# Gated unit of a streaming encoder layer: where ScalarE's operand splits stand among the sigmoids

## The chip, the cores and the metric

The kernel runs on one core of a Trainium2 chip. The metric is the device time of one execution in microseconds. The core has TensorE for matmuls (PE in the profile; PEld is its weight load), VectorE (DVE), ScalarE (ACT), GpSimd (POOL) and SyncE (SP), which here issues the DMAs. Each engine works through its own queue in order.

## The reference

One layer of a hybrid encoder is computed for a prompt of 1024 frames and for 8 x 16 sample frames, 1152 tokens of 1024 features in all. Windowed attention and a state space recurrence (S5) run side by side, and then a convolutional feed-forward network. The change lies in the end of the S5 branch, the gated unit, and in the output projection behind it. Cut to these:

```
z = gelu(y)                                   # (tokens, 512)
s = z * sigmoid(z @ w_glu)                    # w_glu (512, 512)
merged = concat([rmsnorm(a, g_a), rmsnorm(s, g_s)])
x = x + merged @ w_out                        # w_out (1024, 1024)
x = x + conv_ffn(rmsnorm(x))
```

## The kernel before

Everything is float32. Each large product is made of three matmuls on fp32r operands: an operand is split into a high part (a ScalarE copy, rounded to fp32r) and a low part (VectorE, the operand minus its high part), and `mm3` (L60) adds high by high, low weight by high and high by low. In the trace, VectorE's subtraction has line L86, a helper's, and the three matmuls L61, L62 and L63.

The gated unit, `glu(nb)` (L1160), treats the 1152 tokens in three groups of 384. For a group it needs the split of its part of `zT`: `z_tiles` (L942) makes the tiles `zh` and `zlo`, `z_split` (L946) fills them for a slice of the four 128-row blocks, with one ScalarE instruction (L948) and one of VectorE. For each of four output blocks `fo`, 12 matmuls (`pg`) go to a PSUM tile; blocks 0 and 2 use the pool `psc` and blocks 1 and 3 the pool `pat`, two banks each. ScalarE takes the sigmoid of it (`sg`, L1172), which frees the bank; `SG[nb, fo]` keeps that instruction. VectorE multiplies by `zT`, ScalarE makes the high part (`sh`, L1174), VectorE the low part (`sl`), and ScalarE squares (`sqs`, L1177, or in place, L1179), with VectorE adding the squares up. The tile `sg` has two buffers, so the third sigmoid needs the first block's readers to be done. At the end six tiny matmuls (`pss`, L1181) sum the squares into a `psc` bank, and VectorE makes the reciprocal root `rss` from them in twelve small steps.

The first group's splits stand in `y_T` (L995), each behind the gelu of its rows. The second group's tiles lie in a pool of their own, `zl1`; the third group's reuse the first's, in `zl0`.

`load_wo(1, ...)` (L686) makes the operands of the lower half of the output weights: four rows of blocks are loaded (`wor`, tag `xs`, three buffers), and each gives a high part scaled by the norm's gain (`oh`, ScalarE, L704) and a low part (`ol`, VectorE, L705). `wout_s(t)` (L1207) multiplies a tile of 128 tokens by them: two halves of 12 matmuls (`po`) each, evicted by VectorE into the residual `xs` (L1219), then a norm (L1226 to L1229). `h2_T` (L1232) transposes the result (`h2T`) and prepares the operands `hh` of the up-projection (`pu`), whose weights `load_up` (L1276) brings into `ur` and `prep` (L1290) splits into `op`. Those tiles lie where the gated unit's inputs lay.

The text of the program is an order of wishes: the builder's planner puts each engine's instructions in a fixed order of its own, by what is ready when in its plan. `tc.issue_after(ins)` binds it: whatever the block holds for the engine of `ins` (here ScalarE, since `ins` is a sigmoid) is placed behind `ins` in that engine's queue. It adds no wait on the data, and it binds no other engine: VectorE's low parts and SP's loads are free.

The lines around the change are in `emit` itself:

```
    z_tiles(1, zlp)
    for k in range(4):
        z_split(1, slice(k, k + 1))
...
    glu(0)
    with tc.issue_after(SG[0, 0].ins):
        WO[1] = load_wo(1, wop, wk, "xs", 3)
        z_tiles(2, zl0)
        z_split(2, slice(0, 4))
    glu(1)
    glu(2)
```

Of the kernel before, what the change touches and what calls it, by code (L numbers as in the profile page):

```python
# [45 lines left out]
def emit(ctx, tc, x_prompt, x_sample, cache_k, cache_v, state_ssm_re, state_ssm_im, state_conv,  # L46
# [10 lines left out]
    def f(ap):  # L57
        return ap.bitcast(F32)

    def mm3(out, lh, ll, rh, rl, first, last):  # L60
        mm(out, lh, rh, start=first, stop=False, skip_group_check=True)  # L61
        mm(out, lh, rl, start=False, stop=False, skip_group_check=True)  # L62
        return mm(out, ll, rh, start=False, stop=last, skip_group_check=True)  # L63

    def mmf(out, l, r, first=True, last=True):
        mm(out, l, r, start=first, stop=last, skip_group_check=True)

    def pool(name, bufs=1, **kw):
        return tc.tile_pool(name=name, bufs=bufs, reuse_waits="tile", **kw)
# [15 lines left out]
    def tt(o, a, b, op):  # L85
        V_.tensor_tensor(o, a, b, op=op)  # L86
# [23 lines left out]
    def rstd(pl, out, src, width, more=None):  # L110


        n = out.shape[1]
        i = nid()
        a, b, t = (pl.tile([P, n], F32, name=f"rs{c}{i}", tag=f"rs{c}{n}", bufs=1) for c in "abt")
        y = pl.tile([P, n], I32, name=f"rsy{i}", tag=f"rsy{n}", bufs=1)

        def mul(o, x, z, s2=None, op1=None):

            if n == 1:  # L120
                ts(o, x, z, OP.mult, s2, op1)
            else:
                tt(o, x, z, OP.mult)
                if s2 is not None:
                    tt(o, o, s2, op1) if not isinstance(s2, float) else ts(o, o, s2, op1)

        if more is None:
            ts(a, src, 1.0 / width, OP.mult, EPS, OP.add)
        else:
            stt(a, src, 1.0 / width, more, op0=OP.mult, op1=OP.add)  # L130
        ts(y, a.bitcast(I32), -0.5, OP.mult, 1597463007.0, OP.add)
        c = f(y)
        mul(t, c, c, a, OP.mult)
        ts(t, t, -0.5, OP.mult, 1.50087896, OP.add)
        tt(b, c, t, OP.mult)
        mul(t, b, b, a, OP.mult)
        ts(y.bitcast(F32), t, 0.375, OP.mult, -1.25, OP.add)
        mul(t, c, t, 1.875, OP.add)
        tt(out, b, t, OP.mult)
# [546 lines left out]
    def load_wo(part, wp, rawp, tag, bufs):  # L686
        oh = wp.tile([P, 4, DM], F32R, name=f"oh{part}", tag="oh")
        ol = wp.tile([P, 4, DM], F32R, name=f"ol{part}", tag="ol")
        g = consts.tile([P, 4], F32, name=f"og{part}")
        if part == 0:  # L690
            for kv in range(KVH):
                nc.sync.dma_start(g[kv * 64:kv * 64 + 64],
                                  onorm_attn_g[0].rearrange("(k r d) -> k d r", r=RQ, d=HD)[kv])
        else:
            nc.sync.dma_start(g, onorm_ssm_g[0].rearrange("(k p) -> p k", p=P))
        for r in range(4):
            raw = rawp.tile([P, DM], F32, name=f"wor{part}{r}", tag=tag, bufs=bufs)
            if part == 0:
                src = w_out[0, 0:512].rearrange("(k r d) n -> r k d n", r=RQ, d=HD)
                for kv in range(KVH):  # L700
                    nc.sync.dma_start(raw[kv * 64:kv * 64 + 64], src[r, kv])
            else:
                nc.sync.dma_start(raw, w_out[0, 512 + r * P:512 + (r + 1) * P])
            act(oh[:, r], raw, AF.Copy, scale=g[:, r:r + 1])  # L704
            stt(ol[:, r], raw, g[:, r:r + 1], f(oh[:, r]), op0=OP.mult, op1=OP.subtract)  # L705
        return oh, ol
# [235 lines left out]
    def z_tiles(nb, pl):  # L942
        ZH[nb] = pl.tile([P, 4, NBK], F32R, name=f"zh{nb}", tag="zh", bufs=1)
        ZL[nb] = pl.tile([P, 4, NBK], F32R, name=f"zlo{nb}", tag="zl", bufs=1)

    def z_split(nb, ks):  # L946
        tk = slice(nb * NBK, (nb + 1) * NBK)
        act(ZH[nb][:, ks], zT[:, ks, tk], AF.Copy)  # L948
        tt(ZL[nb][:, ks], zT[:, ks, tk], f(ZH[nb][:, ks]), OP.subtract)
# [185 lines left out]
    zl0 = wxa.enter_context(pool("zl0"))  # L1135
# [15 lines left out]
    zl1 = ExitStack()  # L1151
    zlp = zl1.enter_context(pool("zl1", side="right"))
    z_tiles(1, zlp)
    for k in range(4):
        z_split(1, slice(k, k + 1))
    g2 = consts.tile([P, KD], F32, name="g2")
    nc.sync.dma_start(g2, norm2_g[0].rearrange("(k p) -> p k", p=P))
    SB, SG = {}, {}

    def glu(nb):  # L1160
        tk = slice(nb * NBK, (nb + 1) * NBK)
        sh = sgp.tile([P, 4, NBK], F32R, name=f"sh{nb}", tag="sh")
        sl = sgp.tile([P, 4, NBK], F32R, name=f"sl{nb}", tag="sl")
        sqr = sgp.tile([P, NBK], F32, name=f"sqs{nb}", tag="sqs", bufs=1)
        for fo in range(4):
            pl, tg = ((psc, "sc"), (pat, "at"))[fo % 2]
            ps = pl.tile([P, NBK], F32, name=f"pg{nb}{fo}", tag=tg)
            c = slice(fo * P, (fo + 1) * P)
            for k in range(4):
                mm3(ps, gh[:, k, c], gl[:, k, c], ZH[nb][:, k], ZL[nb][:, k], k == 0, k == 3)  # L1170
            sg = sgp.tile([P, NBK], F32, name=f"sg{nb}{fo}", tag="sg")
            SG[nb, fo] = act(sg, ps, AF.Sigmoid)  # L1172
            tt(sg, zT[:, fo, tk], sg, OP.mult)
            act(sh[:, fo], sg, AF.Copy)  # L1174
            tt(sl[:, fo], sg, f(sh[:, fo]), OP.subtract)
            if fo == 0:
                act(sqr, sg, AF.Square)  # L1177
            else:
                act(sg, sg, AF.Square)  # L1179
                tt(sqr, sqr, sg, OP.add)  # L1180
        pss = psc.tile([P, 3], F32, name=f"pss{nb}", tag="sc")  # L1181
        for i in range(3):
            mmf(pss[:, i:i + 1], sqr[:, i * P:(i + 1) * P], ones)
        rss = sgp.tile([P, 3], F32, name=f"rss{nb}", tag="rss")
        rstd(sgp, rss, pss, 512)
        SB[nb] = (sh, sl, rss)
# [72 lines left out]
        nc.gpsimd.tensor_tensor(o, a, b, op=op)  # L1259

    glu(0)
    with tc.issue_after(SG[0, 0].ins):
        WO[1] = load_wo(1, wop, wk, "xs", 3)
        z_tiles(2, zl0)
        z_split(2, slice(0, 4))
    glu(1)
    glu(2)
    zl1.close()
    wxa.close()
# [509 lines left out]
```

## Time and profile before

| | |
|---|---|
| median of 3 runs | 1221.35 us (1220.76 to 1225.33) |
| the profiled execution | 1222.4 us, of which the span of its instructions is 1220.5 |
| mean granted TensorE clock | 0.983 |
| TensorE busy | 1162.7 us, 95% of the span |
| VectorE, ScalarE, GpSimd busy | 940.5, 657.6, 253.6 us |
| first matmul of the gated unit | 342.3 us |
| last matmul of the gated unit | about 397 us |
| TensorE idle from 340 to 460 us, by what it waited for | VectorE's eviction `xs` 5.6 us in 2 waits; `sh` 2.5; `op` 2.3; `st` 1.6; `zT` 1.5 in 2; `sl` 0.8; `sg` 0.6 |

Times in a timeline count from the first instruction. A row has the start, the duration (or the sum of the merged ones, from the first's start to the last's end), the engine, the line, what is written from what, the shape and the count; in brackets stand the idle time of the engine just before and the instruction that ended it. Matmuls overlap, so the distance between two starts, not the duration, is the price of one. The rows of windows hold the busy time of each engine in a stretch, the granted clock, the share of the DMA engines and the bytes per second.

### The profile page before, as it was taken

To read this page: it belongs to the slowest core of one execution; us is meant where nothing else is said; L and a number is where in the kernel's file an instruction comes from. 1 tells how busy PE (TensorE), PEld (TensorE's weight loads), DVE (VectorE), ACT (ScalarE), POOL (GpSimd) and SP (SyncE) were. 2 spreads that over 40 slices of the span, in tenths; PEclk is the share of its full clock that TensorE was granted. 3 is DMA by queue.
4 is the path that set the end of the run, shared out by engine and by line. 5 is a ranking of instruction groups with operands and counts; after the bars stand their busy time and mean duration, and the time that the engine had idled before them with its cause. 6 is when DMAs were issued, how large, how long until landed. Compare 5 with 4: busy or idle time off the path is not lost. (4 is left out here: it accounts for less than half of the span.)

```text
span 1220.5 us, 20645 instructions
## 1 busy us (share of the span) xinstructions
PE 1162.7 (95%) x7396; PEld 1024.4 (84%) x7396; DVE 940.5 (77%) x2058; ACT 657.6 (54%) x1414; POOL 253.6 (21%) x287
## 2 busy tenths in 40 slices
PE   8999999899979887999999999999999998999996
PEld 6777776677769667999999999999999776888885
DVE  6898868797446878887877878878878678977665
ACT  7346556763385766544545445445454555446553
POOL 0000000000000102554454645535443014000000
PEclk9999999999999989999999999999999999999998
DMA  8523236658722421324434334244342799842333
GB/s 264 102 85 123 92 73 195 208 180 234 215 96 86 155 87 52 124 90 143 124 106 145 107 127 140 90 136 132 109 141 99 238 332 343 281 145 94 96 103 138
DMA packets 165032, 177.89 MB, mean 146 GB/s; under 512 B 30618, under 2 KB 122402, under 8 KB 164898
## 3 DMA queue, kind: packets, MB, share of 16 engines
q1 hardware_dynamic: 164930, 176.58, 45.4%
q8 instruction: 58, 0.95, 0.3%
q14 instruction: 44, 0.36, 0.1%
HBM read 124.36 MB, written 53.23 MB: 146 GB/s over the span
## 5 line engine op out<-in xcount | busy, mean ns | idle before, releaser
L1304 DVE TENSOR_TENSOR op<-ur,op 128x512 fp32r<-128x512 f32 x132 | 121.0, 918 | 87.2 <-ACT op L1303 87.1
L1303 ACT ACTIVATE op<-ur 128x512 fp32r<-128x512 f32 x132 | 83.1, 632 | 96.7 <-POOL ur L1259 43.7
L1259 POOL TENSOR_TENSOR S<-ur 128x512 f32<-128x512 f32 x22 | 43.7, 1984 | 242.3 <-DMA ur<-in_w_up_dram 242.1
L1527 ACT ACTIVATE wh<-wd 128x512 fp32r<-128x512 f32 x110 | 68.4, 628 | 26.6 <-PE dnb L63 7.0
L86 DVE TENSOR_TENSOR wl<-wd,wh 128x512 fp32r<-128x512 f32 x110 | 76.3, 704 | 5.9 <-ACT wh L1527 5.7
L62 PE MATMUL dna<-wl,gh 128*128 128x512 f32 x176 | 69.3, 394 | 0.0
L61 PE MATMUL dna<-wh,gh 128*128 128x512 f32 x176 | 64.2, 396 | 3.5 <-ACT wh L1527 3.5
L1392 POOL COPY cvt<-ext 128x2 f32<-128x2 f32 x44 | 30.3, 689 | 158.4 <-DVE ext L86 158.4
L63 PE MATMUL dna<-wh,gl 128*128 128x512 f32 x176 | 54.6, 392 | 0.0
L86 DVE TENSOR_TENSOR gl<-gr,gh 128x512 fp32r<-128x512 f32 x44 | 31.4, 713 | 28.6 <-PE dna L63 12.0
L62 PE MATMUL dnb<-wl,gh 128*128 128x512 f32 x132 | 50.3, 392 | 3.0 <-DVE wl L86 3.0
L86 DVE TENSOR_TENSOR ws<-ws 128x256 f32<-128x256 f32 x88 | 51.8, 589 | 0.7 <-DMA ws<-in_w_down_dram 0.6
L61 PE MATMUL dnb<-wh,gh 128*128 128x512 f32 x132 | 49.0, 392 | 0.6 <-DVE x L86 0.6
L1527 ACT ACTIVATE gh<-gr 128x512 fp32r<-128x512 f32 x44 | 27.6, 630 | 34.7 <-PE dna L62 21.7
L1393 POOL COPY cvt<-ext 128x16 f32<-128x16 f32 x44 | 32.8, 746 | 61.2 <-ACT ext L1363 61.2
L1396 DVE SCALAR_TENSOR_TENSOR cg<-ext,cw,cg 128x1168 f32<-128x1168 f32 x22 | 43.5, 1978 | 0.0
L61 PEld LDWEIGHTS dna<-wh,gh 128*128 128x128 f32 x176 | 33.0, 189 | 11.4 <-ACT wh L1527 4.5
L1527 ACT ACTIVATE gh<-su 128x512 fp32r<-128x512 f32 x33 | 20.9, 632 | 36.8 <-PE dnb L62 13.5
L62 PEld LDWEIGHTS dna<-wl,gh 128*128 128x128 f32 x176 | 33.4, 190 | 7.5 <-DVE wl L86 0.4
L63 PEld LDWEIGHTS dna<-wh,gl 128*128 128x128 f32 x176 | 33.5, 190 | 7.0
L1259 POOL TENSOR_TENSOR ur<-S,ur 128x512 f32<-128x512 f32 x22 | 35.8, 1626 | 17.2 <-DVE op L1304 17.1
L61 PE MATMUL po<-oh,sh 128*128 128x512 f32 x72 | 31.1, 431 | 8.1 <-DVE xs L1219 5.6
(1278 smaller groups left out, 4336.9 us busy)
## 6 DMA issues: line engine op xcount, KB each, us to landing
ur<-in_w_up_dram SPq DMA_DIRECT2D x44, 512.0 KB, 4.7
wd<-in_w_down_dram SPq DMA_DIRECT2D x66, 256.0 KB, 3.5
ws<-in_w_down_dram SPq DMA_DIRECT2D x44, 256.0 KB, 3.4
g_d<-g SPq DMA_DIRECT2D x22, 512.0 KB, 2.6
t_d<-ws SPq DMA_DIRECT2D x22, 512.0 KB, 3.2
gr<-g_d SPq DMA_DIRECT2D x44, 256.0 KB, 6.0
wd<-t_d SPq DMA_DIRECT2D x44, 256.0 KB, 3.0
wa<-a_d SPq DMA_DIRECT2D x9, 512.0 KB, 3.4
```

The lines of the kernel that those rows point to most:

```text
L61: mm(out, lh, rh, start=first, stop=False, skip_group_check=True)
L62: mm(out, lh, rl, start=False, stop=False, skip_group_check=True)
L63: return mm(out, ll, rh, start=False, stop=last, skip_group_check=True)
L86: V_.tensor_tensor(o, a, b, op=op)
L1259: nc.gpsimd.tensor_tensor(o, a, b, op=op)
L1303: act(op[:, 0], src, AF.Copy)
L1304: LOW[n] = V_.tensor_tensor(op[:, 1], src, f(op[:, 0]), op=OP.subtract)
L1392: nc.gpsimd.tensor_copy(cvt[:, 0:2, ft], ext[:, SEQ:SEQ + 2])
L1393: nc.gpsimd.tensor_copy(cvt[:, 2:, ft].rearrange("p (b j) -> p b j", j=2), es[:, :, NS:])
L1396: stt(o, ext[:, 0:GLEN], cw[:, 0, ft:ft + 1], o, op0=OP.mult, op1=OP.add)
L1527: act(hi, src, AF.Copy)
```

## The change

Three blocks of ScalarE and VectorE work are moved in the program's text. The second group's split, four pieces, was traced before the first group's unit and free to run when its data was there; it is now traced behind `glu(0)` and bound behind the second sigmoid of the first group. The output weights' operands were bound behind the first sigmoid and are now bound behind the fourth. The third group's split stood in the same place as the weights, as one instruction for all four row blocks; it now stands behind `glu(1)`, in four pieces, bound behind the second sigmoid of the second group.

```
--- before.py
+++ after.py
@@ -1151,8 +1151,6 @@
     zl1 = ExitStack()
     zlp = zl1.enter_context(pool("zl1", side="right"))
     z_tiles(1, zlp)
-    for k in range(4):
-        z_split(1, slice(k, k + 1))
     g2 = consts.tile([P, KD], F32, name="g2")
     nc.sync.dma_start(g2, norm2_g[0].rearrange("(k p) -> p k", p=P))
     SB, SG = {}, {}
@@ -1259,11 +1257,16 @@
         nc.gpsimd.tensor_tensor(o, a, b, op=op)
 
     glu(0)
-    with tc.issue_after(SG[0, 0].ins):
+    with tc.issue_after(SG[0, 1].ins):
+        for k in range(4):
+            z_split(1, slice(k, k + 1))
+    with tc.issue_after(SG[0, 3].ins):
         WO[1] = load_wo(1, wop, wk, "xs", 3)
-        z_tiles(2, zl0)
-        z_split(2, slice(0, 4))
     glu(1)
+    z_tiles(2, zl0)
+    with tc.issue_after(SG[1, 1].ins):
+        for k in range(4):
+            z_split(2, slice(k, k + 1))
     glu(2)
     zl1.close()
     wxa.close()
```

The functions that the text names, with the lines of the profile:

```
 942    def z_tiles(nb, pl):
 943        ZH[nb] = pl.tile([P, 4, NBK], F32R, name=f"zh{nb}", tag="zh", bufs=1)
 944        ZL[nb] = pl.tile([P, 4, NBK], F32R, name=f"zlo{nb}", tag="zl", bufs=1)
 945
 946    def z_split(nb, ks):
 947        tk = slice(nb * NBK, (nb + 1) * NBK)
 948        act(ZH[nb][:, ks], zT[:, ks, tk], AF.Copy)
 949        tt(ZL[nb][:, ks], zT[:, ks, tk], f(ZH[nb][:, ks]), OP.subtract)
...
1165        for fo in range(4):
1166            pl, tg = ((psc, "sc"), (pat, "at"))[fo % 2]
1167            ps = pl.tile([P, NBK], F32, name=f"pg{nb}{fo}", tag=tg)
1168            c = slice(fo * P, (fo + 1) * P)
1169            for k in range(4):
1170                mm3(ps, gh[:, k, c], gl[:, k, c], ZH[nb][:, k], ZL[nb][:, k], k == 0, k == 3)
1171            sg = sgp.tile([P, NBK], F32, name=f"sg{nb}{fo}", tag="sg")
1172            SG[nb, fo] = act(sg, ps, AF.Sigmoid)
1173            tt(sg, zT[:, fo, tk], sg, OP.mult)
1174            act(sh[:, fo], sg, AF.Copy)
1175            tt(sl[:, fo], sg, f(sh[:, fo]), OP.subtract)
1176            if fo == 0:
1177                act(sqr, sg, AF.Square)
1178            else:
1179                act(sg, sg, AF.Square)
1180                tt(sqr, sqr, sg, OP.add)
```

## The prediction

> **What bounds the kernel now.** I read the page first, then the engines' timelines around the gated unit, then its windows.
>
> ```profile
> span 1220.5 us, 20645 instructions
> PE 1162.7 (95%) x7396; PEld 1024.4 (84%) x7396; DVE 940.5 (77%) x2058; ACT 657.6 (54%) x1414; POOL 253.6 (21%) x287
> ```
>
> TensorE is busy for 95% of the span, so a change off TensorE can only return time in which TensorE stands still or runs slowly. The place of this change is the stretch from 351 to 380 us. The windows there (columns: busy us of PE, PEld, DVE, ACT and POOL with their instruction counts, granted clock, DMA share, GB/s):
>
> ```profile
> 356.00:358.00 2.00, 1.37 (x8) 1.07 (x7) 1.07 (x3) 1.99 (x4) 0.00 (x0) 1.00 0.00 0
> 360.00:362.00 2.00, 0.17 (x1) 0.17 (x2) 2.00 (x3) 2.00 (x3) 0.00 (x0) 1.00 0.77 250
> 364.00:366.00 2.00, 2.00 (x5) 1.61 (x6) 2.00 (x4) 0.86 (x3) 0.00 (x0) 0.50 0.64 260
> ```
>
> While ScalarE is full, TensorE does 0.17 of 2 us, and then runs at half clock (0.50). TensorE's timeline (start, duration, what, idle before and its releaser):
>
> ```profile
> 351.69 0.97 PE L61 MATMUL pg<-zh,gh 128*128 128x384 f32 x4
> 355.97 0.34 PE L63 MATMUL pg<-zh,gl 128*128 128x384 f32 x1
> 356.94 0.44 PE L61 MATMUL pg<-zh,gh 128*128 128x384 f32 x1 [0.63 <-ACT sg L1172]
> 361.83 0.50 PE L61 MATMUL po<-oh,sh 128*128 128x512 f32 x1 [2.52 <-ACT sh L1174]
> 363.82 0.79 PE L63 MATMUL po<-oh,sl 128*128 128x512 f32 x1 [0.79 <-DVE sl L86]
> 372.21 0.72 PE L66 MATMUL pss<-ones,sqs 128*128 128x1 f32 x6
> 372.80 0.42 PE L61 MATMUL pg<-zh,gh 128*128 128x384 f32 x1
> 379.01 0.34 PE L63 MATMUL pg<-zh,gl 128*128 128x384 f32 x1
> 379.19 0.40 PE L61 MATMUL po<-oh,sh 128*128 128x512 f32 x1
> 384.56 0.40 PE L63 MATMUL po<-oh,sl 128*128 128x512 f32 x1
> ```
>
> The first two rows are the first and the last of the 24 matmuls with which the first token group ends: four at once, then five for each of the four blocks. The last ends at about 356.15. From there to 379.19 TensorE does five output blocks of the gated unit (60 matmuls `pg`), both halves of the first output tile (24 matmuls `po`) and the six tiny `pss`. Their price without stalls: 36 `pg` lie between 372.80 and 379.01, 6.21/35 = 0.177 us each, so a block of 12 costs 2.13; 24 `po` from 379.19 to 384.56, 5.37/23 = 0.233 each, 5.60; `pss` 372.80 - 372.21 = 0.59. Sum: 10.64 + 5.60 + 0.59 = 16.8 us. It takes 379.19 - 356.15 = 23.0. **So 6.2 us are lost here**: 0.63 + 2.52 + 0.79 = 3.94 idle, and the other 2.3 at half clock and in refilling. That is all that the change can return in this stretch, 0.51% of the time. A measurement of this kernel can tell about 0.5%, 6.1 us, from no change.
>
> Why TensorE waits is on ScalarE's timeline:
>
> ```profile
> 351.12 0.52 ACT L948 ACTIVATE zh<-zT 128x384 fp32r<-128x384 f32 x1
> 352.93 1.77 ACT L948 ACTIVATE zh<-zT 128x384 fp32r<-128x384 f32 x4 [1.29 <-DMA out_dram<-fo]
> 354.72 1.28 ACT L1172 ACT_TABLE_LOAD   x1
> 356.01 0.87 ACT L1172 ACTIVATE sg<-pg 128x384 f32<-128x384 f32 x2
> 356.77 3.23 ACT L704 ACTIVATE oh<-wor,og 128x1024 fp32r<-128x1024 f32 x3
> 359.89 1.48 ACT L948 ACTIVATE zh<-zT 128x1536 fp32r<-128x1536 f32 x1
> 361.26 0.52 ACT L1174 ACTIVATE sh<-sg 128x384 fp32r<-128x384 f32 x1
> 361.67 0.51 ACT L1177 ACTIVATE sqs<-sg 128x384 f32<-128x384 f32 x1
> 362.81 1.15 ACT L704 ACTIVATE oh<-wor,og 128x1024 fp32r<-128x1024 f32 x1 [0.20 <-DMA wor<-in_w_out_dram]
> 363.86 0.49 ACT L1172 ACTIVATE sg<-pg 128x384 f32<-128x384 f32 x1
> 366.40 0.49 ACT L1172 ACTIVATE sg<-pg 128x384 f32<-128x384 f32 x1
> 375.19 0.87 ACT L1172 ACTIVATE sg<-pg 128x384 f32<-128x384 f32 x2 [5.96 <-PE pg L63]
> ```
>
> Five matmuls take 0.885, so the first group's blocks finish at about 353.5, 354.4, 355.3 and 356.15. But the first two sigmoids stand behind the second group's split (352.93, itself held by an output DMA) and the table load, and the third and fourth behind three `oh`, the third group's split, and `sh`. They run at 363.86 and 366.40. Four PSUM banks serve the unit, so TensorE gets only the bank of one early sigmoid for a block of the second group (356.94) and then has nothing to do.
>
> **The change part by part.** It adds and removes no arithmetic but three `zh` and three `zlo` instructions: the third group's split becomes four pieces, 1.77 us of ScalarE in place of 1.48 (both rows above), 0.3 more, hidden while ScalarE has its 5.96 us idle before 375.19; without that cover it costs 0.3. VectorE does likewise:
>
> ```profile
> 353.49 1.97 DVE L86 TENSOR_TENSOR zlo<-zT,zh 128x384 fp32r<-128x384 f32 x4 [0.98 <-ACT zh L948]
> 357.95 3.68 DVE L705 SCALAR_TENSOR_TENSOR ol<-wor,og,oh 128x1024 fp32r<-128x1024 f32 x3 [0.39 <-ACT oh L704]
> 359.27 0.34 SPq L703 DMA_DIRECT2D wor<-in_w_out_dram  x1
> 496.38 1.28 ACT L1401 ACT_TABLE_LOAD   x1
> 498.05 1.18 ACT L1401 ACTIVATE cg<-cg 128x1168 f32<-128x1168 f32 x1 [0.39 <-DVE cg L1396]
> ```
>
> *Second group's split behind the second sigmoid.* The table load no longer follows it. The last two rows show that a table load runs ahead of its activation's wait: it ended at 497.66, and the Silu behind it then waited another 0.39 for VectorE. So the load can run from 351.64 (end of the last first-group split) to 352.9, under TensorE's work. The first sigmoid starts with its data, at 353.7 with some latency, instead of 356.01, the second at about 354.6, ending 355.1. The four split pieces follow at 0.44 each (1.77/4), to 356.85; the first `zlo` ends near 356.2 (355.1, one piece of 0.51 by the square of the same shape at 361.67, and about 0.55 by the `zlo` row). TensorE, free at 356.15, waits about 0.1 in place of 0.63, and each later piece arrives faster (0.44) than its three matmuls run (0.53). The wait for the output DMA at 352.93 is past by then, and what is late next is the bank for the second block.
>
> *Weights' operands behind the fourth sigmoid, third split behind the second group's second.* Now `sh`, square and `sh` (pitch 361.67 - 361.26 = 0.41) follow the pieces from 356.85, and the third sigmoid, which needs a `sg` buffer that the first block's low part gives back, runs at about 358.1 to 358.55: the second block of the second group starts at 358.6 rather than 358.4. The fourth follows near 359.65 to 360.1, before TensorE needs its bank at 360.7. The third block ends near 362.8 (358.6 and twice 2.13). Until here 0.1 for the `zlo` and 0.2 to 0.3 for the bank are lost; I take 0.3 for the latter.
>
> What the wait pushes back is the weights. They are queued behind the fourth sigmoid: first `oh` at 360.1 instead of 356.77. Three raw buffers are loaded early; the fourth load waits for the first `ol`. Before, that `ol` ended at 359.23 (357.95 + 3.68/3, overlapped), SP issued at 359.27, and the fourth `oh` started at 362.81, 3.58 after. Now: `oh` 360.1 to 361.25, `ol` to 362.5, load landed 366.1, fourth `oh` 367.25, fourth `ol` 368.5. TensorE begins `po` at 362.8 and is through three quarters by 367.0; the matmuls with the fourth `ol` wait about 1.5. SP itself is not delayed for others: behind the fourth `wor` it has the residual loads, which are needed only at the eviction. Bounds of this term: 0, if a block of the gated unit lies in between; and 4, if the four remaining `sh` and squares (0.43 each, 1.7) run ahead of `oh` too and the longer gap brings half clock (0.7). I take 1.6, near the middle chain, since the load's 3.58 is measured and its start is bounded by the sigmoid.
>
> Whether such a gap brings half clock is in these rows:
>
> ```profile
> 455.07 0.41 PE L61 MATMUL pu00c<-hh,op 128*128 128x320 f32 x1 [2.29 <-ACT op L1303]
> 457.74 0.47 PE L61 MATMUL pu00c<-hh,op 128*128 128x320 f32 x1
> 458.01 0.47 PE L62 MATMUL pu00c<-hl,op 128*128 128x320 f32 x1
> ```
>
> After 2.29 us of idleness the matmuls run at a pitch of 0.27 (458.01 - 457.74) where 320 columns at the `pg` rate would be 0.15. So a gap of 2.3 us can do it, and one of 1.6 is taken as free. [...]
>
> **Sum.** Lost now 6.2; lost after 0.1 + 0.3 + 1.6 = 2.0, bounds 0.2 and 4.3. Gain 4.2 us, between 1.9 and 6.0. The profiled execution's own time is 1222.4 (span 1220.5 and 1.9 around it): 1218.2. The median of the three runs is 1221.35, 1.05 below that execution, so I forecast 1217.2 for the median.
>
> Does it reach the end? These rows decide:
>
> ```profile
> 397.29 1.79 ACT L1255 ACTIVATE hh<-st 128x896 fp32r<-128x896 f32 x2 [1.56 <-PE pg L63]
> 412.17 1.15 ACT L1303 ACTIVATE op<-ur 128x512 fp32r<-128x512 f32 x2 [3.37 <-DMA ur<-in_w_up_dram]
> 419.14 0.66 PE L1241 MATMUL h2T<-ident,h 128*128 128x128 f32 x4 [1.60 <-ACT st L1249]
> 422.51 0.80 PE L61 MATMUL po<-oh,sh 128*128 128x512 f32 x1 [2.71 <-DVE xs L1219]
> 400.00:410.00 10.00, 10.00 (x44) 8.03 (x43) 10.00 (x28) 8.34 (x20) 0.00 (x0) 1.00 0.30 116
> ```
>
> The next stage's first operand (397.29) waits for the last `pg` on TensorE, and the up weights' buffers lie where the unit's inputs lay, so what follows should start as much earlier as TensorE finishes the unit.
>
> **The rivals.**
> 1. *Absorbed.* VectorE is full from 400 to 410 (10.00 of 10) and TensorE waits for it at 422.51 (2.71). If VectorE, which now does splits and weights later, paces that stretch, the 4.2 us come back as a longer wait there: 1221.4. Against it: the row at 397.29 shows that stretch opened by TensorE. Chance 0.13.
> 2. *More than the stretch.* The builder's planner orders all engines anew; if the evictions come earlier at 422.51, part of 1.60 + 2.71 idle there and of the half clock behind it (2.3 as above) goes too. Half of 6.6 on top of 4.2 gives 7.5: 1213.9. Nothing in the rows asks for it; chance 0.20.
> 3. *Slower: the second group's split comes too late.* The edge orders it only behind the second sigmoid; the planner may put the first group's remaining `sh`, squares and sigmoids (two sigmoids, four `sh`, four squares, about 4.8 us with their waits on VectorE) and three `oh` (3.23) ahead of it. Before, it put three `oh` and a split ahead of an `sh` traced earlier, so program order does not protect. Then the first `zlo` ends at 364.1 (356.2 + 4.8 + 3.2, rounded), TensorE is idle for 8.0 and loses 2.3 at half clock: 10.3 against 6.2, slower by 4.1, 1225.4. It decides from the point where idle plus 2.3 exceeds 6.2, a first `zlo` later than 360.05. [...] Against this rival: the weights' edge is two sigmoids further back than the split's. Chance 0.12.
>
> A reordering that I don't foresee, slower by over 0.5%: 0.03.
>
> **How the numbers follow.** The forecast case has 0.52, of which I count 0.05 beyond 6.1 us since its best bound is 6.0. Faster: 0.05 + 0.20 = 0.25. Slower: 0.03 and 0.05 of the third rival's 0.12 (its price with a late `po` on top) = 0.08. Same: 0.47 + 0.13 + 0.07 = 0.67. The forecast case alone spans 1215.4 to 1219.5. The range of 1212.8 to 1224.0 takes in that, the first rival and most of the second, and leaves out about 0.17.
>
> **What would show it.** Right: the table load directly behind the split at about 351.6; the first sigmoid near 353.8; TensorE's idle time before the second group's first block below 0.2; no 2.5 us gap and a clock of 1.00 from 356 to 362; the fourth `oh` near 366 with a wait for its load, and `po` waiting 1 to 2 us; the mark "24th `po` done and five blocks done" near 375 instead of 379.2; the row at 397.29 about 4 us earlier. Wrong: a first `zlo` after 360; TensorE's gaps at 419 and 422 grown by what was won; or `po` queued ahead of the second group's blocks, so that the late weights stop them too.

## The result, and the profile after

| | before | after |
|---|---|---|
| median, runs side by side | 1222.99 us (8 runs, 1220.76 to 1227.37) | 1216.92 us (8 runs, 1214.07 to 1218.57) |
| ratio | | 0.9943, 95% interval 0.9929 to 0.9956 |
| profiled execution, span | 1220.5 us | 1216.2 us (time 1217.9) |

A second set of runs of the changed kernel, beside the last experiments, gave 0.9931 (0.9912 to 0.9949). By the ratio the change takes 7.0 us off (5.4 to 8.7 by the interval, from 1223), where 4.2 had been forecast; the two medians lie 6.1 apart. Most of the gain is not in the place where the forecast looked for it.

To see where it is I cut every profile into five stages by five marks on TensorE: the last matmul of the first token group's unit, the last matmul `pg` of the unit, the first `pu10a` (the up-projection's second round), the first `dna` (the down-projection) and the end. In some kernels nine more `po` are done before the last `pg`; 0.233 us for each is moved from the unit to the projection.

| us | start to unit | unit | output projection | up-projection | down-projection |
|---|---|---|---|---|---|
| before | 355.97 | 40.90 | 92.42 | 468.01 | 263.19 |
| after | 357.17 | 39.45 | 87.03 | 468.05 | 264.46 |
| after, second profile | 355.18 | 39.53 | 86.95 | 468.11 | 262.58 |

The first and the last stage hold none of the TensorE work that the change touches, and they scatter by some us between profiles of the same kernel (357.17 and 355.18; 264.46 and 262.58). Unit, output projection and up-projection repeat within 0.1 in these two profiles. **The unit gives 1.4 us, the output projection 5.4**, together 6.8, which fits the measured 7.0.

The page of after:

```profile
span 1216.2 us, 20649 instructions
PE 1161.7 (96%) x7396; PEld 1022.7 (84%) x7396; DVE 943.3 (78%) x2061; ACT 658.2 (54%) x1417; POOL 256.6 (21%) x287
```

The unit on TensorE's timeline (start, duration, line, tiles, shape, count, and in brackets the idle time before and what ended it). All times are 1.2 us later than before, because the stages ahead of it took longer in this execution:

```profile
357.17 0.34 PE L63 MATMUL pg<-zh,gl 128*128 128x384 f32 x1
358.33 0.44 PE L62 MATMUL pg<-zlo,gh 128*128 128x384 f32 x1 [0.30 <-DVE zlo L86]
362.45 0.45 PE L61 MATMUL pg<-zh,gh 128*128 128x384 f32 x1 [1.92 <-ACT sg L1170]
369.61 0.73 PE L61 MATMUL po<-oh,sh 128*128 128x512 f32 x2 [0.58 <-ACT oh L704]
370.93 0.50 PE L62 MATMUL po<-ol,sh 128*128 128x512 f32 x1 [0.59 <-DVE ol L705]
377.03 0.39 PE L61 MATMUL po<-oh,sh 128*128 128x512 f32 x1
```

From the end of the first group (357.17 + 0.17) to 377.03 TensorE does 49 `pg`, 24 `po` and the six `pss`: 49 x 0.177 + 24 x 0.233 + 0.59 = 14.85 us of work in 19.69. So 4.8 us are lost where it was 6.2; 3.4 of them are the four waits in brackets, and the rest lies in slower starts around them (0.42 us from 357.17 to the next `pg`, 0.29 from the one at 362.45, where 0.177 is usual). The 2.5 us wait for `sh` has gone, but a new one of 1.92 us stands before the second block, for a sigmoid. ScalarE in the same stretch:

```profile
354.96 1.28 ACT L1170 ACT_TABLE_LOAD   x1 [2.14 <-PE pg L63]
356.25 0.88 ACT L1170 ACTIVATE sg<-pg 128x384 f32<-128x384 f32 x2
357.01 1.76 ACT L948 ACTIVATE zh<-zT 128x384 fp32r<-128x384 f32 x4
360.26 0.49 ACT L1170 ACTIVATE sg<-pg 128x384 f32<-128x384 f32 x1 [0.25 <-DVE sl L86]
361.91 0.49 ACT L1170 ACTIVATE sg<-pg 128x384 f32<-128x384 f32 x1
362.30 3.22 ACT L704 ACTIVATE oh<-wor,og 128x1024 fp32r<-128x1024 f32 x3
368.40 1.15 ACT L704 ACTIVATE oh<-wor,og 128x1024 fp32r<-128x1024 f32 x1 [2.06 <-DMA wor<-in_w_out_dram]
```

ScalarE has nothing to do for 2.14 us, and the table load starts only when the first block is done. With four sigmoid buffers, in a later experiment, the same load runs at 350.70, 2.07 us ahead of its sigmoid. The queue's order is what the change asked for: two sigmoids, the four split pieces, the other two sigmoids (360.26, 361.91), then the weights. The 1.92 us wait ends with the sigmoid at 361.91, the fourth. The clock (the column behind the five engines) stays at 1.00 where the kernel before had 0.50:

```profile
360.00:362.00 2.00, 0.54 (x4) 0.21 (x2) 1.71 (x5) 1.54 (x5) 0.00 (x0) 1.00 0.00 0
364.00:366.00 2.00, 2.00 (x11) 1.78 (x10) 2.00 (x3) 2.00 (x4) 0.00 (x0) 1.00 0.14 16
```

Now the output projection. Rows 419.14 and 422.51 of before, in the prediction, are two of its waits there; a third is this one:

```profile
440.97 0.50 PE L61 MATMUL po<-oh,sh 128*128 128x512 f32 x1 [2.90 <-DVE xs L1219]
```

That makes 1.60 + 2.71 + 2.90 = 7.2 us of idleness. After has 4.7 in its three waits of this stretch:

```profile
418.04 0.50 PE L61 MATMUL po<-oh,sh 128*128 128x512 f32 x1 [0.80 <-DVE xs L1217]
424.62 1.09 PE L1239 MATMUL h2T<-ident,h 128*128 128x128 f32 x8 [0.72 <-ACT h L1227]
428.86 0.50 PE L61 MATMUL po<-oh,sh 128*128 128x512 f32 x1 [3.15 <-DVE xs L1217]
```

The rest of the 5.4, 2.9 us, is by my estimate what the clock behind the waits makes: 1.00 minus the clock, added up over the windows of 4 us from 412 to 448, comes to 5.2 us before, a part of it while TensorE waits, and to 1.7 after. Two of these windows of before, then two of after:

```profile
424.00:428.00 4.00, 4.00 (x11) 3.02 (x10) 1.39 (x7) 2.08 (x4) 0.00 (x0) 0.50 0.30 124
440.00:444.00 4.00, 3.03 (x10) 2.42 (x11) 3.73 (x15) 3.27 (x5) 0.00 (x0) 0.78 0.50 141
```

```profile
420.00:424.00 4.00, 3.90 (x17) 2.82 (x15) 4.00 (x19) 3.31 (x5) 0.00 (x0) 1.00 0.32 131
428.00:432.00 4.00, 3.14 (x9) 2.53 (x10) 3.71 (x14) 3.03 (x5) 0.00 (x0) 0.73 0.52 192
```

Up to about 450 us before had two episodes of half clock and after has one; behind that both have two more (from about 455 and 476 us before, 450 and 471 after). Why TensorE waited at 422.51 is on VectorE's timeline of before. Token tile 5 is multiplied in two halves, and the banks are free only when VectorE has evicted them (`xs<-po`):

```profile
416.64 0.16 DVE L83 TENSOR_SCALAR rsa<-pss 128x3 f32<-128x3 f32 x1 [0.36 <-PE pss L66]
416.84 1.26 DVE L83 TENSOR_SCALAR rsy<-rsa 128x3 int32<-128x3 int32 x1
418.13 0.16 DVE L86 TENSOR_TENSOR rst<-rsy 128x3 f32<-128x3 f32 x1
418.33 1.12 DVE L86 TENSOR_TENSOR rst<-rst,rsa 128x3 f32<-128x3 f32 x1
419.68 1.11 DVE L86 TENSOR_TENSOR rsb<-rsy,rst 128x3 f32<-128x3 f32 x1
421.71 1.40 DVE L1219 SCALAR_TENSOR_TENSOR xs<-po,rss,xs 128x512 f32<-128x512 f32 x2
```

The evictions at 421.71 stand behind most of the third token group's norm, twelve tiny steps on 128x3 elements that begin with `rsa<-pss` when the `pss` behind both halves are done. Three of these steps took over 1.1 us instead of 0.16. GpSimd at that time:

```profile
416.81 1.27 POOL L1259 TENSOR_TENSOR ur<-ur,ur 128x512 f32<-128x512 f32 x1
418.15 1.28 POOL L1259 TENSOR_TENSOR ur<-S,ur 128x512 f32<-128x512 f32 x1
419.51 1.27 POOL L1259 TENSOR_TENSOR ur<-ur 128x512 f32<-128x512 f32 x1
```

Each long step ends with an operation of GpSimd: 416.84 + 1.26 = 418.10 and 416.81 + 1.27 = 418.08; 419.45 and 419.43; 420.79 and 420.78. In the whole trace of before the median of each of these three steps is 0.15 to 0.16 us. Two of them (`rst<-rst,rsa` and `rsb<-rsy,rst`) have two inputs, the third has one; `rst<-rst,rsa` once more, at 421.03, when the last of these operations was done, took 0.16. So the rows show that the steps and the operations end together; how one holds the other they do not show. Not every step is held: three `TENSOR_SCALAR` steps of one column ran in their usual 0.15 to 0.28 us between 415.57 and 416.28, while GpSimd worked from 415.45 for 1.27 us.

After evicts tile 5 earlier, at 417.23 and 419.92, before the norm:

```profile
417.23 0.75 DVE L1217 SCALAR_TENSOR_TENSOR xs<-po,rss,xs 128x512 f32<-128x512 f32 x1 [1.26 <-PE po L63]
419.92 0.73 DVE L1217 SCALAR_TENSOR_TENSOR xs<-po,rss,xs 128x512 f32<-128x512 f32 x1
420.84 0.15 DVE L83 TENSOR_SCALAR rsa<-pss 128x3 f32<-128x3 f32 x1
```

From these rows came two theories. **A: two gains.** The unit's 1.4 us come from the order on ScalarE, and the projection's 5.4 from another order of work on VectorE and TensorE around tile 5, which the planner chose when the third split moved. **B: one gain.** The earlier sigmoids start everything behind them earlier, and the projection only passes it on, its work meeting other work in another phase.

### The profile page after: what moved, and what is told of

Same layout as the page of the kernel before. It is cut to its first block, busy times and chain, and to the rows that moved or that the text cites. A ratio compares the mean times of both kernels' runs of the same rounds, so it can differ in the third digit from the quotient of the medians.

```text
span 1216.2 us, 20649 instructions
## 1 busy us (share of the span) xinstructions
PE 1161.7 (96%) x7396; PEld 1022.7 (84%) x7396; DVE 943.3 (78%) x2061; ACT 658.2 (54%) x1417; POOL 256.6 (21%) x287
## 5 line engine op out<-in xcount | busy, mean ns | idle before, releaser
L86 DVE TENSOR_TENSOR ws<-ws 128x256 f32<-128x256 f32 x88 | 56.1, 637 | 0.8 <-DVE ext L86 0.4
```

## Experiments: one part at a time

Four kernels, all made from the kernel before. The first three each make one of the three moves alone.

The second group's split alone:

```
@@ -1154,2 +1154,0 @@
-    for k in range(4):
-        z_split(1, slice(k, k + 1))
@@ -1261,1 +1259,4 @@
     glu(0)
+    with tc.issue_after(SG[0, 1].ins):
+        for k in range(4):
+            z_split(1, slice(k, k + 1))
```

> Only the second group's split is moved behind the second sigmoid; weights and third split stay as before. In the built program TensorE's order is that of the kernel before in the unit and in the output projection alike. Theory A (two separate gains: about 1.4 us in the unit from moving the weights and the split off the sigmoids, about 5.4 us in the output projection from another order of its work, which the third split's move brings): 0 to 1 us, ratio 0.999 to 1.001. Theory B (one gain: sigmoids earlier in the unit, and all the rest, the projection too, follows from arriving earlier): the first sigmoids come about 1 us earlier, so 1 to 3 us, ratio 0.9975 to 0.999.

The weights' operands alone:

```
@@ -1262,2 +1262,3 @@
-    with tc.issue_after(SG[0, 0].ins):
+    with tc.issue_after(SG[0, 3].ins):
         WO[1] = load_wo(1, wop, wk, "xs", 3)
+    with tc.issue_after(SG[0, 0].ins):
         z_tiles(2, zl0)
```

> Only the weights' operands are moved behind the fourth sigmoid; the splits of both groups stay as before. TensorE's order is that of the changed kernel in the unit and that of the kernel before in the output projection. Theory A: 1 to 2 us, ratio 0.998 to 0.9993, and the projection's waits for evictions (2.71 and 2.90 us) stay. Theory B: this is most of the unit's change, so 4 to 7 us, ratio 0.994 to 0.997.

The third group's split alone:

```
@@ -1263,3 +1263,6 @@
         WO[1] = load_wo(1, wop, wk, "xs", 3)
-        z_tiles(2, zl0)
-        z_split(2, slice(0, 4))
     glu(1)
+    z_tiles(2, zl0)
+    with tc.issue_after(SG[1, 1].ins):
+        for k in range(4):
+            z_split(2, slice(k, k + 1))
```

> Only the third group's split is moved, in four pieces behind the second group's second sigmoid; the second split and the weights stay as before. TensorE's order is that of the kernel before in the unit and that of the changed kernel in the output projection. Theory A: the unit still loses about 5 to 6 us, the projection is short: 4 to 6 us in all, ratio 0.995 to 0.997. Theory B: the long waits for the third and fourth sigmoid remain but for one split, so 0 to 1.5 us, ratio 0.9988 to 1.000.

The fourth leaves all three as they were and moves only the third group's norm (its `pss`, L1181, and the twelve steps behind it) to the place behind tile 5's evictions:

```
+        def norm():
             pss = psc.tile([P, 3], F32, name=f"pss{nb}", tag="sc")
...
+        if nb < 2:
+            norm()
+        else:
+            LATE.append(norm)
...
-            stt(x[:, d], ps, rss[:, i:i + 1], x[:, d], op0=OP.mult, op1=OP.add)
+            EV[t] = stt(x[:, d], ps, rss[:, i:i + 1], x[:, d], op0=OP.mult, op1=OP.add)
...
         wout_s(t)
+        if t == 5:
+            with tc.issue_after(EV[5].ins):
+                LATE[0]()
```

> The kernel before, with the gated unit untouched; only the third group's norm (six tiny matmuls and twelve small VectorE steps) is traced and bound behind the last eviction of the sixth token tile on VectorE, where the kernel before has it ahead of both evictions of that tile. Theory A: TensorE's wait of 2.71 us at the seventh tile and the half clock behind it go or shrink: 2 to 5 us, ratio 0.996 to 0.9985. Theory B: nothing in the unit comes earlier, so no change, 0.9995 to 1.001.

The results of all eleven experiments and of the repeated kernel stand in one table. "Stages" is the change in unit, projection and up-projection together against the profile of before; "measured" is the ratio's distance from 1 times 1223 us, with its interval. The stages come from one profile of each kernel. The down-projection is left out of them: six kernels (weights alone, third split alone, norm late alone, norm first, and the two with four buffers and no new tile) have another order on TensorE there, and take 262.4 to 266.8 us in it, against 262.6 to 265.9 in the other eight profiles.

| | ratio | unit | projection | up | stages, us | measured, us |
|---|---|---|---|---|---|---|
| before | 1 | 40.90 | 92.42 | 468.01 | 0 | 0 |
| after | 0.9943 | 39.45 | 87.03 | 468.05 | -6.8 | -7.0 (-8.7 to -5.4) |
| after again | 0.9931 | 39.53 | 86.95 | 468.11 | -6.7 | -8.4 (-10.8 to -6.2) |
| second split alone | 1.0012 | 41.45 | 92.11 | 467.99 | +0.2 | +1.5 (-0.5 to 3.3) |
| weights alone | 1.0016 | 40.83 | 92.28 | 467.94 | -0.3 | +2.0 (0.1 to 3.9) |
| third split alone | 0.998 | 41.66 | 87.81 | 468.01 | -3.9 | -2.4 (-4.3 to -0.6) |
| norm late, nothing else | 0.9965 | 41.31 | 88.51 | 467.94 | -3.6 | -4.3 (-6.1 to -2.4) |
| after, early table load, new tile | 0.9971 | 38.48 | 87.78 | 470.28 | -4.8 | -3.5 (-5.9 to -1.3) |
| after, four sigmoid buffers | 0.994 | 37.17 | 86.64 | 468.27 | -9.3 | -7.3 (-9.5 to -5.3) |
| after, norm first | 1.002 | 39.54 | 94.12 | 468.09 | +0.4 | +2.4 (0.6 to 4.3) |
| after, both and norm late, new tile | 0.9947 | 37.31 | 86.67 | 470.31 | -7.0 | -6.5 (-8.8 to -4.3) |
| after, early table load in place | 0.9929 | 38.67 | 88.34 | 467.94 | -6.4 | -8.7 (-10.8 to -6.6) |
| after, four buffers and early load in place | 0.9924 | 36.58 | 87.18 | 468.28 | -9.3 | -9.3 (-11.9 to -6.6) |
| after, new tile only | 0.9982 | 39.56 | 87.74 | 470.40 | -3.6 | -2.2 (-3.9 to -0.5) |

B falls: the norm moved alone wins 3.9 us in the projection with the unit untouched (0.4 slower), and the third split alone wins 4.6 there with a unit that is 0.8 slower. Two of the three moves, alone, leave the projection where it was. In the instruction lists of the built programs the projection's part is the same before, with the second split alone and with the weights alone; it is changed, in the same way, in after and with the third split alone. So the projection's gain comes with the third split's move. Its size is less sharp than the 5.4 of one pair of profiles: the three profiles with the old order have 92.1 to 92.4 us, the six with the new one 87.0 to 88.3, so it is 3.8 to 5.5.

Not all forecasts of time came true. The weights alone were to win 1 to 2 us by A and 4 to 7 by B, and came out 2.0 slower (0.1 to 3.9); the stages show none of that. The third split alone was to win 4 to 6 us by A; its stages show 3.9, its time 2.4 (0.6 to 4.3).

The unit's gain is not a sum of parts, which theory A had missed. Alone, the moves give +0.55, -0.07 and +0.76 us, together -1.45. TensorE's largest wait in each, in the order of the experiments:

```profile
363.65 0.50 PE L61 MATMUL po<-oh,sh 128*128 128x512 f32 x1 [3.21 <-ACT sh L1172]
```

```profile
361.41 0.45 PE L61 MATMUL pg<-zh,gh 128*128 128x384 f32 x1 [3.42 <-ACT sg L1172]
```

```profile
361.62 0.50 PE L61 MATMUL po<-oh,sh 128*128 128x512 f32 x1 [1.14 <-ACT sh L1174]
367.58 0.50 PE L61 MATMUL po<-oh,sh 128*128 128x512 f32 x1 [2.14 <-ACT sh L1174]
```

With one block of work taken out of the sigmoids' way another stays in it: without the weights' move the three `oh` stand ahead of `sh`, and with it alone the splits stand ahead of the sigmoids. Of the kernels run, only those with all three moves gain in the unit; two moves at a time were not run.

How the late norm wins is less simple than theory A had it. VectorE's timeline, then TensorE's:

```profile
420.48 1.10 DVE L86 TENSOR_TENSOR st<-st 128x128 f32<-128x128 f32 x1 [1.73 <-ACT st L1256]
421.50 1.40 DVE L1226 SCALAR_TENSOR_TENSOR xs<-po,rss,xs 128x512 f32<-128x512 f32 x2
```

```profile
421.02 1.11 PE L1248 MATMUL h2T<-ident,h 128*128 128x128 f32 x4 [2.67 <-ACT st L1256]
422.30 0.80 PE L61 MATMUL po<-oh,sh 128*128 128x512 f32 x1 [0.16 <-DVE xs L1226]
430.70 1.09 PE L1248 MATMUL h2T<-ident,h 128*128 128x128 f32 x8 [0.19 <-ACT h L1236]
```

The evictions no longer stand behind the norm, but behind a subtraction that waits for ScalarE, and come 0.2 us earlier than before (1.0 counted from the last `pg`). The first two waits shrink from 4.3 to 2.8 us, and the third, 2.90 at 440.97, is gone, since the work behind stands in another order too. In return the wait for `op` grows from 2.29 (455.07 before) to 3.75. What the run shows is that the place of the norm, with the order that the planner makes around it, is enough to win 3.9 us here without any move of a split; that its three stretched steps alone cost the time is not shown.

## Experiments: what is left in the unit, and the norm put back

All four start from the kernel after. In the first, a tiny sigmoid (one column) is bound behind the first group's last split, and the real sigmoids behind it, so that the table is loaded early. It writes to a new four-byte tile:

```
+    warm = consts.tile([P, 1], F32, name="warm")
+    with ExitStack() as late:
+        for k in range(4):
+            late.enter_context(tc.issue_after(ZS[0, k].ins))
+        WARM = act(warm, ones, AF.Sigmoid)
...
-            SG[nb, fo] = act(sg, ps, AF.Sigmoid)
+            with tc.issue_after(WARM.ins):
+                SG[nb, fo] = act(sg, ps, AF.Sigmoid)
```

> The changed kernel with one tiny sigmoid put behind the first group's last split, so that the activation table (1.28 us) is loaded before the first block's data are there; TensorE's order is that of the changed kernel. Theory 'load on the path' (the load waits in ScalarE's queue with its sigmoid, and the first sigmoid starts a whole load late): the first sigmoid starts about 1.3 us earlier against the end of its block, and so do the other three, the bank wait of 1.92 us before block 0 shrinks to 0.6 to 0.9 or goes, and the unit's stretch is 1.0 to 1.3 us shorter than after; time against before 0.992 to 0.994. Rival 'covered' (the fourth weight load is the last thing that TensorE waits for, whatever the sigmoids do): the wait for the operands grows by what the bank wait loses, the stretch stays within 0.4 us, ratio as after, 0.993 to 0.996.

In the second, the sigmoids have four buffers:

```
+    sgl = zl1.enter_context(pool("sgl", 4, side="right"))
...
-            sg = sgp.tile([P, NBK], F32, name=f"sg{nb}{fo}", tag="sg")
+            sg = sgl.tile([P, NBK], F32, name=f"sg{nb}{fo}", tag="sg")
```

> The changed kernel with four buffers for the sigmoids instead of two, so that the third and the fourth need not wait for the first two blocks' low parts and squares. In its order the third norm stands ahead of tile 5's evictions again, as in the kernel before. Theory 'the order of norm and evictions makes the projection's gain': the unit's stretch is 0.5 to 2 us shorter than after, the projection stage loses 3 to 5 us of its 5.4, and the time is 0.995 to 0.999 of before. Rival 'the third split's place itself makes the projection's gain, by what it takes off VectorE before 400 us': the projection keeps its 5.4 and the ratio is 0.992 to 0.994.

In the third, tile 5's evictions are bound behind the third norm again; `RN[2]` is the norm's last step:

```
-            stt(x[:, d], ps, rss[:, i:i + 1], x[:, d], op0=OP.mult, op1=OP.add)
+            with tc.issue_after(RN[2].ins) if t == 5 else ExitStack():
+                stt(x[:, d], ps, rss[:, i:i + 1], x[:, d], op0=OP.mult, op1=OP.add)
```

> The changed kernel with one edge more: both evictions of tile 5 stand behind the third token group's norm on VectorE, as they did before; the unit is the changed kernel's. Theory 'the order of norm and evictions makes the projection's gain': the projection stage is 2 to 5 us longer than after, the unit and all else as after, ratio 0.996 to 0.9995. Rival 'the third split's place itself': the projection stays within 1 us of after, ratio 0.993 to 0.9955.

The fourth has the early table load, the four buffers and the late norm together:

```
+        WARM = act(warm, ones, AF.Sigmoid)
...
+    sgl = zl1.enter_context(pool("sgl", 4, side="right"))
...
+            with tc.issue_after(EV[5].ins):
+                LATE[0]()
```

> The changed kernel with the early table load, the four sigmoid buffers, and the third norm put behind tile 5's evictions. Both theories of the unit's waits: no bank wait for a sigmoid is left, unit 1 to 3 us shorter than after. Projection by 'order of norm and evictions': 3.5 to 5.5 us shorter than before. Ratio 0.991 to 0.994; if the stage behind 'the fourth weight load' takes all of the unit's gain, 0.994 to 0.996.

*The norm put back.* The projection takes 94.12 us instead of 87.03, and the whole gain is gone (1.002). It lost more than the 2 to 5 us expected, because the transposes now wait, first of all, and long:

```profile
422.45 1.97 PE L1240 MATMUL h2T<-ident,h 128*128 128x128 f32 x8 [5.63 <-ACT h L1228]
426.86 1.97 PE L1240 MATMUL h2T<-ident,h 128*128 128x128 f32 x8 [2.45 <-ACT h L1228]
```

The evictions of tile 5 on VectorE stand right behind the norm's last step:

```profile
426.49 1.40 DVE L1218 SCALAR_TENSOR_TENSOR xs<-po,rss,xs 128x512 f32<-128x512 f32 x2
```

They come at 426.49, against 421.71 in the kernel before, so this is not the old order again, and its 7.1 us are no measure of the 5.4. But the third split is in its new place here, and all the stage's gain is lost: that place alone does not make it.

*Four buffers.* The expectation was that the projection would lose, since the norm again stands ahead of the evictions in this program. It did not: 86.64. VectorE's timeline shows why:

```profile
412.16 0.14 DVE L83 TENSOR_SCALAR rsa<-pss 128x3 f32<-128x3 f32 x1
414.63 0.16 DVE L86 TENSOR_TENSOR rss<-rsb,rst 128x3 f32<-128x3 f32 x1
417.22 1.41 DVE L1218 SCALAR_TENSOR_TENSOR xs<-po,rss,xs 128x512 f32<-128x512 f32 x2 [1.66 <-DMA xs<-xa_d]
```

Here the `pss` stand between the two halves of tile 5 on TensorE, so the norm starts earlier, runs from first to last step in 2.6 us (7.4 in the kernel before, 416.64 to 424.05), with no step stretched, and is done 2.4 us before the evictions, which wait for their residual from DRAM. In its numbers (86.64 and a ratio of 0.994) the run came out as the rival had said and not as the theory. So theory A's wording falls: a norm ahead of the evictions need not cost anything. The rival alone falls too, by the late norm, which wins without the split's move, and by the norm put back. What fits all of these kernels is whether the norm's steps still hold VectorE when TensorE needs a bank; no run changes that and nothing else, so it stays argued.

The same kernel shows what held the table load. ScalarE's timeline:

```profile
350.70 1.28 ACT L1171 ACT_TABLE_LOAD   x1
352.77 0.49 ACT L1171 ACTIVATE sg<-pg 128x384 f32<-128x384 f32 x1 [0.79 <-PE pg L63]
```

Here the load runs ahead of its sigmoid, as the prediction had it for the changed kernel. The instruction lists of the two programs differ in what each of the two waits for (the changed kernel, then four buffers). Waits that the builder writes as instructions of their own are listed with the instruction behind them:

```
396 L1170 ACT_TABLE_LOAD [waits PE_49]
397 L1170 ACTIVATE sg00_4406<-pg00_4393 128x384 [waits Pool_49]

396 L1171 ACT_TABLE_LOAD [waits DMAHW0_49,DMAHW1_49,DVE_49]
397 L1171 ACTIVATE sg00_4409<-pg00_4396 128x384 [waits PE_49]
```

In both lists one wait stands with the sigmoid and the others in front of the load. In the changed kernel the one on TensorE went there; with another buffer for `sg` it stayed with the sigmoid.

*Worth of each.* The early load shortens the unit by 1.0 us (39.45 to 38.48). Theory "load on the path" had 1.0 to 1.3, but also that the bank wait of 1.92 would shrink; it stayed at 1.96, since TensorE no longer waits for `zlo` either (0.30 in after) and comes to the bank earlier. Four buffers take the wait away altogether (no row of TensorE between 354 and 364 us has one) and the unit to 37.17. The time with the early load, 0.9971, missed both forecasts (0.992 to 0.994 and 0.993 to 0.996); the up-projection, below, is part of that.

*All three together* have a unit of 37.31 and a projection of 86.67, the same as with four buffers alone, where the load runs early anyway.

*What was not expected.* Both kernels with the early load have an up-projection of 470.3 us, where all the others have 467.9 to 468.3, with TensorE busy throughout between 500 and 900 us and its granted clock at 1.00 in both cases.

## Experiments: the added tile, and the best version

The early load again, without a new tile: the tiny sigmoid writes a column of the squares' tile, which is overwritten later.

```
         sqr = sgp.tile([P, NBK], F32, name=f"sqs{nb}", tag="sqs", bufs=1)
+        if nb == 0:
...
+                WARM.append(act(sqr[:, 0:1], ones, AF.Sigmoid))
```

> The changed kernel with the early table load as in the earlier run of it, but the tiny sigmoid writes into a column of the squares' tile that is overwritten later, so that no tile is added and every address stays. That run's up projection took 470.3 us where eight others took 468.0. Theory 'the added four-byte tile shifted the addresses behind it': up projection 468.0, unit about 1 us shorter than after, ratio 0.992 to 0.9945. Rival 'the early sigmoid itself, or chance': up projection again 470.3 or in between, ratio 0.995 to 0.998.

The same with the four buffers:

```
+    sgl = zl1.enter_context(pool("sgl", 4, side="right"))
...
+                WARM.append(act(sqr[:, 0:1], ones, AF.Sigmoid))
```

> The changed kernel with four sigmoid buffers and the early table load in place. Theory 'four buffers alone already let the table load run early' (in that run the load stood right behind the last split): the unit stays within 0.4 us of the run with four buffers alone, ratio 0.992 to 0.995. Rival 'the load still costs there': unit 0.7 to 1.3 us shorter still, ratio 0.991 to 0.993.

The changed kernel with the tile alone:

```
+    warm = consts.tile([P, 1], F32, name="warm")
+    V_.memset(warm, 0.0)
```

> The changed kernel with nothing but a four-byte tile more among the constants, set to zero once. Theory 'addresses': up projection 470.3 us instead of 468.0, everything else as after, ratio 0.9955 to 0.9975. Rival: up projection 468.0, ratio 0.993 to 0.9955.

And the changed kernel once more, with no edit.

> The changed kernel once more, beside the others on the same chip. All theories: 0.993 to 0.9956 of before; the second profile shows how far stages scatter between executions: projection within 1 us of 87.0, unit within 0.5 of 39.4, up projection 468.0, down projection 262 to 267.

The tile alone brings the 2.3 us, and without it they are gone (467.94). The two marks on TensorE of the kernel with the tile, and of after:

```profile
485.65 0.31 PE L61 MATMUL pu10a<-hh,op 128*128 128x320 f32 x1
956.05 1.20 PE L61 MATMUL dna<-wh,gh 128*128 128x512 f32 x4 [1.97 <-ACT wh L1532]
```

```profile
483.64 0.31 PE L61 MATMUL pu10a<-hh,op 128*128 128x320 f32 x1
951.69 1.74 PE L61 MATMUL dna<-wh,gh 128*128 128x512 f32 x4 [1.85 <-ACT wh L1530]
```

956.05 - 485.65 = 470.40 against 951.69 - 483.64 = 468.05. But for the one memset, the instructions of the two built programs are the same and stand in the same order on every engine; most tiles lie 32 bytes higher. So addresses are the difference that is left; which of them, and how they cost 0.5% of the stage, stays open. The kernel with the tile missed its forecast in time (0.9955 to 0.9975 expected, 0.9982 measured): its median is 6.3 us above that of after in the same set of runs, 1221.53 against 1215.19, and this stage explains 2.35 of it. Where the rest lies stays open; one profile each, whose first and last stages scatter by as much, can't tell.

Without the tile, the early load's unit is 38.67, 0.8 us shorter than after. Its wait for the bank is the same as with the tile (1.95 and 1.96 us). Behind the one with the tile a `pg` takes 0.34 us; here, from the fifth matmul on, it takes 0.52, and the next one starts 0.32 us later instead of 0.18:

```profile
357.38 0.45 PE L61 MATMUL pg<-zh,gh 128*128 128x384 f32 x1 [1.95 <-ACT sg L1176]
359.20 0.52 PE L62 MATMUL pg<-zlo,gh 128*128 128x384 f32 x1
```

Four buffers and the early load give the shortest unit, 36.58, 2.9 us less than after and 0.6 less than with four buffers alone. That lies between the two expectations (within 0.4, and 0.7 to 1.3), so whether the load still costs there is not settled. Its ratio to before is 0.9924 (0.9903 to 0.9946), beside 0.9931 (0.9912 to 0.9949) for the changed kernel on the same chip: by its stages it is the better version, but these runs can't tell the two apart.

## Why the prediction was right in its number and wrong in its reasons

The forecast was 1217.2 and the time 1216.92. That they agree so closely is luck. Two terms were wrong in opposite directions: the unit gave 1.4 us where 4.2 had been forecast, 2.8 too few, and the output projection 5.4 where the forecast had none. That leaves 2.6 us more gain than forecast by the stages; 1.6 of them don't show in the time because the median of before was 1222.99 over more runs, not 1221.35, and the rest is within the scatter of single executions.

- *The loss of 6.2 us*, and that ScalarE's order causes it: right. The wait of 2.52 us for `sh` went, and with it the half clock (0.50 from 364 to 366 us before, 1.00 after).
- *"A table load runs ahead of its activation's wait"*: wrong here. The Silu row showed one load that stood ahead of its activation's wait; in this place the wait for TensorE stands ahead of the load. The first sigmoid starts at 356.25, where the block's last matmul released ScalarE at 354.96. The forecast sum goes without these 1.3 us from the first sigmoid on. The load takes 1.28 us in both places, and the sigmoid starts right at its end (354.96 + 1.28 = 356.24).
- *The bank, 0.3 us*: mis-sized, 1.92. The forecast let the second block of the second group take the third sigmoid's bank. The program has blocks 0 and 2 in one pool of two banks, with the `pss`, and blocks 1 and 3 in the other, and TensorE's list has blocks 1 and 3 first; so the second block waits for the fourth sigmoid. That sigmoid came at 361.91, which is 1.1 us later than the forecast's 359.65 moved by this execution's 1.2. The pools, by `fo % 2`, were to be had from the code.
- *A gap of 2.3 us brings half clock, one of 1.6 is free*: the length alone does not decide. Behind a wait of 1.92 us the clock stayed at 1.00 here and a `pg` took 0.34; behind one of 1.95 in the early load without a tile it took 0.52.
- *The first `zlo`, 0.1*: 0.30 idle. *The fourth load, 1.6*: right as a mechanism. The fourth `oh` was forecast at 367.25, with the 1.2 at 368.45, and started at 368.40; TensorE's two waits for it are 0.58 + 0.59 = 1.17, less than forecast because it came to it late.
- *Sum of the unit*: lost after 4.8, not 2.0; the forecast's upper bound was 4.3, and the 0.7 in it for half clock was an estimate that no row gives (the clock stayed at 1.00 from 356 to 374 us). It failed by the load and the bank: with the early load and four buffers the unit is 2.9 us shorter still, which leaves a loss of 1.9, about the forecast's 2.0.
- *"What follows should start as much earlier as TensorE finishes the unit"*: right for what the unit gave, but blind to the second source.
- *Second rival, "more than the stretch", 0.20*: this is what happened, though not as "half of 6.6 on top of 4.2". It said that nothing in the rows asks for it. Its own rows hinted at it: 2.71 us of waiting for an eviction, on a VectorE that was full from 400 to 410. What was missing was a look at which instructions stood between the last `po` of tile 5 and its eviction. And the third wait, 2.90 at 440.97, with its own half clock, was left out of the 6.6.
- *First rival, "absorbed"*: no sign; the projection got shorter. *Third rival, split too late*: the pieces followed right behind the second sigmoid (357.01), `zlo` cost 0.30.

The chance of 0.25 for faster by more than 0.5% was low for a ratio of 0.9943, and 0.9931 in the second set of runs.

## What to carry to other kernels

Where a planner orders the queues anew, a moved block can win or lose more in the next stage than in its own: look ahead for the places where TensorE waits for an eviction, and ask what stands in front of it on VectorE and whether that order can flip. Before counting on a freed bank, follow which pool's bank the waiting block takes and which instruction frees just that one. And compare stages between marks, not only times: the up-projection's 2.3 us showed in single profiles here, where single times scatter by 5. But a stage with waits scatters too: the projection, in one and the same order, took 87.0 to 88.3.

## What was not expected of the hardware

- Where the table load stood behind its activation's wait for TensorE, its whole 1.28 us came after the data were there: it ran at 354.96 with 2.14 us of idleness before it. In the program with four buffers it ran at 350.70 with none.
- The length of a wait does not alone decide how fast TensorE goes on: behind waits of 1.92 (after, clock 1.00) and 1.96 us (early load with the new tile) a `pg` took 0.34, behind one of 1.95 at the same place (early load without the tile) 0.52. Behind one of 3.15 (after) the clock was 0.59 from 430 to 434 us.
- Three tiny VectorE steps took 1.11 to 1.26 us instead of 0.16 beside GpSimd's operations of 1.27 to 1.28, each ending within 0.02 us of one of them; others in the same stretch took their usual 0.15 to 0.28.
- A four-byte tile more made an up-projection of 468.0 us take 470.3 to 470.4, in three kernels of three.
